# First feed-forward layer by one level of Strassen, second layer in column halves, w_out by token sets

## The chip, the cores and the metric

The kernel runs on one core of one Trainium2 chip. The metric is device time in microseconds (us) of one execution, the median of 3 runs: 1400.36 us for the kernel before (1397.95 to 1401.98). Engines are named as the profile names them: PE (TensorE, matrix products), PEld (its weight loads), DVE (VectorE), ACT (ScalarE), POOL (GpSimd), SP (SyncE, which only issues DMAs here).

## What is computed

One layer of a hybrid decoder on 1024 prompt tokens and 8 sample tokens with the same weights, 1032 tokens together. All data is float32; the model is 1024 wide, the feed-forward layer 2816.

```python
def hybrid_layer(x, h_re, h_im, cbuf, p):
    xn = rmsnorm(x, g_mix)
    z = xn @ w_in
    u, cv, cg = z[..., :512], z[..., 512:1024], z[..., 1024:1536]
    gates = jax.nn.sigmoid(z[..., 1536:])
    y, hr, hi = s5_layer(u, h_re, h_im, ...)
    yg = jax.nn.gelu(y) @ w_glu
    ya = yg[..., :D_MODEL] * jax.nn.sigmoid(yg[..., D_MODEL:])
    c, new_buf = causal_dwconv(cv * jax.nn.sigmoid(cg), cbuf, conv_w, conv_b)
    yb = jax.nn.silu(layernorm(c, ln_g, ln_b)) @ w_pw
    merged = gates[..., :D_MODEL] * ya + gates[..., D_MODEL:] * yb
    x = x + merged @ w_out
    hn = rmsnorm(x, g_ffn) @ w_ff_in
    x = x + (jax.nn.silu(hn[..., :D_FF]) * hn[..., D_FF:]) @ w_ff_out
    return x, hr, hi, new_buf
```

A last rmsnorm with g_final follows. The change touches the last four lines.

## The kernel before

Activations lie transposed, 128 features on the partitions and the 1032 tokens along the free dimension. A factor of a product is scaled by a power of two and split into two float16 numbers, high and low; a product is three passes of matmuls (high by high, weights high by activations low, weights low by activations high), added up in PSUM. `lin` does this for one output tile of 128 features: `wdma` loads the raw weights on SP's queue into one of 3 buffers (`wr`), `wscale` finds the scale (ACT squares and sums, L513; POOL takes the maximum over partitions, L518; DVE makes a power of two, L523, L497, L498, and `invs` its inverse, L508), `wsplit16` splits (ACT makes the high half, L558, DVE the low one, L562), and `mtile` issues the matmuls (L591), three column pieces of 344 for each k and pass, into one of two PSUM buffers of three banks (`mm`).

The stages in order: norm and S5 layer, the input projections, the convolution, the gates with `pw(m)` for m = 0 to 7 (product with w_pw, gating, merged rows `mg`). Then come `wout(m)` and `residual(m)`. `wout` loads and splits one tile of w_out; `residual` loads a tile of x as tokens by features and transposes it on PE (`pxt`, L1084, L1087), and ACT copies it from PSUM (L1085, L1088). The merged rows are split into `mh`. `out(c)` does w_out for one of three column groups of 384, 384 and 264 tokens: `mcol` issues the matmuls (L1120), DVE adds the residual (L1143), squares are summed, and `put` scales by the reciprocal root and by g_ffn (L1156) and splits into `xg` (L1158, L1159).

`ff_in(n)` makes one of 22 tiles of hidden rows: two products of 8 k by 3 passes by 3 pieces, 144 matmuls, with weights of the gate and of the linear half, a sigmoid on ACT (L1206), two multiplications on DVE (L1207, L1210), and a sum of squares. n = 0 is issued by column groups, so that it can begin while `out` ends. The hidden rows of a block are split by `hsplit` when all of them are there, and then used by the second layer: for each m one `lin` over the block's rows, added to `x1` on DVE (L1261). `FBLK` gives the hidden tiles of each of 5 blocks. The first n of the next block is issued between `hsplit` and the second layer of a block. The last block's product (`pfo`, L1278) is done by three column groups with the transposes of the output (`tr`, L1287) and the last norm (L1290 on ACT, L1297 on DVE) behind each.

Each engine works in order. A scheduler sets that order from the program's order; `hp()` and `high_priority` move instructions ahead of others, HPS = 20000 further than HPO = 3000.

Of the kernel before, what the change touches and what calls it, by code (L numbers as in the profile page):

```python
# [437 lines left out]
def hybrid_step(ctx: ExitStack, tc: tile.TileContext, x_prompt, x_sample, state_ssm_re, state_ssm_im,  # L438
# [673 lines left out]
    B3 = (0, 3 * P, 6 * P, TOK)  # L1112
    K3 = ((0, 1, 2), (3, 4, 5), (6, 7, 8))
    G3 = ((0, 1, 2), (3, 4, 5), (6, 7))

    def mcol(w, acts, o):
        n = len(acts)
        for k in range(n):
            for i, (a, b) in enumerate(((0, 0), (0, 1), (1, 0))):
                T.matmul(o, w[a][:, k], acts[k][b], start=(k == 0 and i == 0), stop=(k == n - 1 and i == 2))  # L1120

    wo, so = [], cp.tile([P, 8], F32, name="so")

    def wout(m):
        raw = wdma(w_out, 0, 8, m * P)
        t = pair(sa("wo", (P, 2, 8, P), F16))
        s = wscale([raw], [t[0]], so[:, m:m + 1])
        wo.append(wsplit16(raw, t[0], t[1], s))

    xg = []  # L1130

    def out(c):
        a, b = B3[c], B3[c + 1]
        w = b - a
        inv = io
        sq = sb("sq", (P, 384), tag="t")
        for gr in G3:
            pt = mpsum()
            for i, m in enumerate(gr):
                mcol(wo[m], [(h[:, a:b], l[:, a:b]) for h, l in mh], pt[:, i, :w])  # L1140
                x = x1[m][:, a:b]
                with hp():
                    V.scalar_tensor_tensor(x, pt[:, i, :w], inv[:, m:m + 1], x, MUL, ADD)  # L1143
                    if m == 0:
                        A.activation(sq[:, :w], x, AF.Square)
                    else:
                        t = sb("sqt", (P, 384), tag="t")
                        A.activation(t[:, :w], x, AF.Square)
                        V.tensor_tensor(sq[:, :w], sq[:, :w], t[:, :w], ADD)
        if c == 0:  # L1150
            xg.extend(pair(sb("xgp", (P, 2, TOK), F16, tag="mg")) for _ in range(8))

        def put(o, p):
            for m in range(8):
                t = sb("xgt", (P, 384), tag="t")
                V.scalar_tensor_tensor(t[:, :w], x1[m][:, a:b], gff[:, m:m + 1], p, MUL, MUL)  # L1156
                h, l = xg[m]
                A.copy(h[:, a:b], t[:, :w])  # L1158
                V.tensor_tensor(l[:, a:b], t[:, :w], h[:, a:b], SUB)  # L1159
# [4 lines left out]
    for m in range(3):
        wout(m)
    for m in range(4):
        residual(m)
    mh = [pair(sa("mh", (P, 2, TOK), F16) if m < 5 else sb("mh", (P, 2, TOK), F16, tag="gy")) for m in range(8)]
    with hp():
        msc, mcx = ascale(mss, "msc")  # L1170
        for c in range(3):
            for m in range(8):
# [3 lines left out]
    for m in range(3, 8):  # L1176
        wout(m)
        if m < 7:
            residual(m + 1)
# [156 lines left out]
```

## Time and profile before

| | |
|---|---|
| runs | 1400.36 us median, 1397.95 to 1401.98 |
| profiled execution | 1400.05 us, of it span 1398.3 us |
| mean granted clock of PE | 0.974 |

The span by stages, as the view of windows gives it: the first two columns are the window and its length, then busy us of PE, PEld, DVE, ACT and POOL with the number of instructions, the granted clock of PE as a share of full speed, the DMA engines' busy share, and GB/s.

```profile
85.00:450.00 365.00, 332.92 (x2226) 231.88 (x2226) 310.28 (x595) 145.04 (x265) 38.00 (x64) 0.95 0.39 93
450.00:554.00 104.00, 104.00 (x715) 69.83 (x714) 54.50 (x85) 45.38 (x58) 5.99 (x10) 1.00 0.23 67
704.00:1346.00 642.00, 642.00 (x4389) 430.04 (x4387) 249.32 (x497) 216.38 (x313) 31.33 (x80) 1.00 0.17 50
1346.00:1398.00 52.00, 40.48 (x293) 29.33 (x291) 34.56 (x126) 9.47 (x18) 0.00 (x0) 0.94 0.21 82
```

The windows end where the work changes: the gates and w_pw from 450 to 554 us, w_out with n = 0 of the first layer from there to 704, both feed-forward layers to 1346, the last block's second layer with the output behind it. In a row of the timeline the first number is the start, the second the duration; in a group of instructions the two numbers behind the first bar are busy us in all and the mean ns of one, and behind the second bar stands the idle time ahead of them with what ended it.

### The profile page before, as it was taken

To read this page: it belongs to the slowest core of one execution; us is meant where nothing else is said; L and a number is where in the kernel's file an instruction comes from. 1 tells how busy PE (TensorE), PEld (TensorE's weight loads), DVE (VectorE), ACT (ScalarE), POOL (GpSimd) and SP (SyncE) were. 2 spreads that over 40 slices of the span, in tenths; PEclk is the share of its full clock that TensorE was granted. 3 is DMA by queue.
4 is the path that set the end of the run, shared out by engine and by line. 5 is a ranking of instruction groups with operands and counts; after the bars stand their busy time and mean duration, and the time that the engine had idled before them with its cause. 6 is when DMAs were issued, how large, how long until landed. Compare 5 with 4: busy or idle time off the path is not lost.

```text
span 1398.3 us, 22132 instructions
## 1 busy us (share of the span) xinstructions
PE 1303.8 (93%) x8877; PEld 892.6 (64%) x8877; DVE 800.6 (57%) x1830; ACT 535.3 (38%) x882; POOL 98.9 (7%) x208
## 2 busy tenths in 40 slices
PE   3898798999998999599989999999999999999996
PEld 2776565666665666367656666666666666666665
DVE  5976888989996635646532433335432434342547
ACT  5834333453334434822332422324232422342412
POOL 5000001100010000000000000000000000000100
PEclk9999899999998999799999999999999999999999
DMA  7445754341121115320011112111221112110103
GB/s 191 126 96 119 141 109 107 99 115 37 55 63 45 31 57 145 117 61 1 1 50 51 29 54 76 46 41 32 65 62 54 29 54 76 46 49 27 50 27 122
DMA packets 168976, 96.45 MB, mean 69 GB/s; under 512 B 12799, under 2 KB 165003, under 8 KB 168873
## 3 DMA queue, kind: packets, MB, share of 16 engines
q1 hardware_dynamic: 167469, 92.44, 24.3%
q0 software_dynamic: 896, 1.63, 0.6%
q8 instruction: 69, 1.13, 0.3%
q10 hardware_dynamic: 507, 0.97, 0.3%
q14 instruction: 35, 0.28, 0.1%
HBM read 76.72 MB, written 9.65 MB: 62 GB/s over the span
## 4 chain that ended last, share of the span: by engine, by line
PE 70%; DVE 14%; issue 9%; DMA 3%; ACT 1%; POOL 1%; SPq 1%; DVEq 0%; ACTq 0%; POOLq 0%
PE mm L591 57%; PE mm L1120 7%; DVE acc L895 3%; PE pfo L1278 2%; PE pu L731 2%; DVE wl L562 2%; DMA Y<-X 1%; DVE tb L895 1%; POOL sv L518 1%; DMA U<-ud 1%; DVE mg L968 1%; DMA M<-kvd 1%; DVE mg L965 0%; DVE xgt L1156 0%; PE ptr L721 0%
## 5 line engine op out<-in xcount | busy, mean ns | idle before, releaser
L591 PEld LDWEIGHTS <-wh 128*128 128x128 f16 x4656 | 457.5, 98 | 234.2 <-issue 5.4
L591 PE MATMUL mm<-xgp,wh 128*128 128x344 f16 x2016 | 350.6, 310 | 4.5 <-DVE py L497 4.5
L591 PEld LDWEIGHTS <-wl 128*128 128x128 f16 x2328 | 228.8, 98 | 112.3 <-issue 0.8
L513 ACT ACTIVATE wh<-wr 128x1024 bf16<-128x1024 f32 (+2 forms) x114 | 109.1, 957 | 407.0 <-PE mm L591 264.4
L591 PE MATMUL mm<-xn,wh 128*128 128x344 f16 (+2 forms) x1152 | 205.6, 313 | 1.9 <-ACT ut L743 1.1
L591 PE MATMUL mm<-xgp,wl 128*128 128x344 f16 x1008 | 202.7, 310 | 0.0
L562 DVE SCALAR_TENSOR_TENSOR wl<-wr,wsc,wh 128x1024 f16<-128x1024 f32 (+2 forms) x112 | 129.8, 1160 | 63.7 <-ACT wh L558 61.2
L558 ACT ACTIVATE wh<-wr,wsc 128x1024 f16<-128x1024 f32 (+2 forms) x112 | 117.0, 1045 | 116.5 <-DVE wsc L498 109.4
L591 PE MATMUL mm<-hp,wh 128*128 128x344 f16 x912 | 157.8, 309 | 0.0
L518 POOL PARTITION_ALL_REDUCE sv<-wss x124 | 67.1, 541 | 1088.6 <-ACT wh L513 1038.8
L523 DVE TENSOR_SCALAR sv<-sv 128x1 f32<-128x1 f32 x124 | 18.9, 152 | 180.7 <-POOL sv L518 180.7
L591 PE MATMUL mm<-xn,wl 128*128 128x344 f16 (+2 forms) x576 | 118.7, 313 | 0.0
L1210 DVE SCALAR_TENSOR_TENSOR g<-mm,inv,g 128x1032 f32<-128x1032 f32 x21 | 27.2, 1293 | 127.2 <-PE mm L591 127.2
L1120 PE MATMUL mm<-mh,wo 128*128 128x384 f16 (+1 forms) x576 | 90.3, 319 | 3.9 <-DVE x L1143 2.8
L591 PE MATMUL mm<-hp,wl 128*128 128x344 f16 x456 | 91.3, 309 | 0.0
L1261 DVE SCALAR_TENSOR_TENSOR x<-mm,inv,x 128x1032 f32<-128x1032 f32 x32 | 41.3, 1292 | 72.3 <-PE mm L591 72.3
L1120 PEld LDWEIGHTS <-wo 128*128 128x128 f16 x576 | 57.7, 101 | 35.3 <-issue 8.9
L591 PE MATMUL mm<-gyp,wh 128*128 128x344 f16 x384 | 66.6, 309 | 1.4 <-DVE mg L968 0.8
L895 DVE SCALAR_TENSOR_TENSOR acc<-t,cws,acc 128x511 f32<-128x511 f32 (+14 forms) x60 | 44.9, 749 | 0.0
L895 DVE SCALAR_TENSOR_TENSOR acc<-c,cw,acc 128x511 f32<-128x511 f32 (+14 forms) x60 | 43.6, 746 | 0.0
L591 PE MATMUL mm<-gyp,wl 128*128 128x344 f16 x192 | 38.4, 309 | 0.0
L1278 PE MATMUL pfo<-hp,wlp 128*128 128x392 f16 (+2 forms) x216 | 34.1, 309 | 0.0
(379 smaller groups left out, 1401.5 us busy)
## 6 DMA issues: line engine op xcount, KB each, us to landing
wr<-in_w_ff_in_dram SPq DMA_DIRECT2D x44, 512.0 KB
wr<-in_w_in_dram SPq DMA_DIRECT2D x28, 512.0 KB
wr<-in_w_ff_out_dram SPq DMA_DIRECT2D x24, 320.0 KB
...
```

The lines of the kernel that those rows point to most:

```text
L513: A.activation(junk, src, AF.Square, accum_out=o)
L518: GP.partition_all_reduce(v, ss, P, RMAX)
L523: V.tensor_scalar(v, v, 1e-28, None, MAXI)
L558: A.mul(hi, raw, s)
L562: V.scalar_tensor_tensor(lo[:, sl], raw[:, sl], s, hi[:, sl], MUL, SUB)
L591: T.matmul(pt[:, c, :b - a], ww[:, k], aa[:, a:b], start=(k == 0 and i == 0), stop=(k == n - 1 and i == 2))
L731: T.matmul(o, ww[:, k], aa[:, c0:c0 + w], start=(k == 0 and i == 0), stop=(k == 7 and i == 2))
L895: V.scalar_tensor_tensor(o[:, q:], x[:, 0:HT - q], w[q], o[:, q:], MUL, ADD)
L1120: T.matmul(o, w[a][:, k], acts[k][b], start=(k == 0 and i == 0), stop=(k == n - 1 and i == 2))
L1210: V.scalar_tensor_tensor(c3(g1), z, inv, c3(g1), MUL, MUL)
L1261: V.scalar_tensor_tensor(c3(x1[m]), z, inv, c3(x1[m]), MUL, ADD)
L1278: T.matmul(pt[:, :w], wl[m][a][:, k], hid[k][b][:, c0:c0 + w], start=(k == 0 and i == 0), stop=(k == nb - 1 and i == 2))
```

## The change

**w_out.** `wout(0)` to `wout(3)` and `residual(0)` to `residual(3)` are issued inside the pw loop, and all eight split tiles stay in SBUF. The PSUM pool `mm` ends behind the pw loop; three buffers of two banks (`mq`) take its place. The 1032 tokens are seen as two halves of 516. A token set j is 129 tokens of the first half and the same 129 of the second, 258 columns in a matmul; `msplit(j)`, `out(j)` and `xsplit(j)` split, multiply and rescale one set. `xsplit` also forms the sums of activations that Strassen needs, and splits all into float16 tiles `xs`.

**First layer.** The two output tiles of one n (gate, linear) by the two halves of the tokens, with the 1024 features as two halves of 512, make a 2 by 2 block product. `ff_in` does it by 7 products in place of 8: `ff_prep` forms four sums of weight blocks on DVE and splits seven blocks of 512; `prod` issues 4 k by 3 passes by 2 pieces of 258 columns, 24 matmuls; DVE adds the products into the hidden tiles (L1270), ACT copies the first (L1298). n = 0 does two column pieces, 387 and 129 of each half.

**Second layer.** Two halves of 516 columns in pieces of 258. The blocks change, the first n of the next block comes ahead of `hsplit`, and some tags get other buffers. The factor of a bound (32, now 64) allows for the sums.

```diff
+    def wout(m):
+        raw = wdma(w_out, 0, 8, m * P)
...
     def pw(m):
...
-        with hp():
+        with tc.high_priority(offset=HPS if m == 7 else HPO):
...
         pw(m)
+        if 2 <= m < 6:
+            wout(m - 2)
+        if m >= 4:
+            residual(m - 4)
+    emm.close()
+    emq = ctx.enter_context(ExitStack())
+    mq = emq.enter_context(tc.tile_pool(name="mq", bufs=3, space=bass.MemoryType.PSUM))
...
+    msplit(0)
+    for m in range(4, 8):
+        residual(m)
+    for m in range(4, 8):
+        wout(m)
...
+    def out(j):
+        n = 2 * (SETS[j + 1] - SETS[j])
+        ms_ = (5, 4, 6, 7, 0, 1, 2, 3) if j else range(8)
+        for i in range(4):
+            pt = qpsum()
+            for b in range(2):
+                m = ms_[2 * i + b]
...
+                o = v2(pt[:, b, :n])
+                for k in range(8):
+                    for q, (u, v) in enumerate(((0, 0), (0, 1), (1, 0))):
+                        T.matmul(o, wo[m][u][:, k], cset(mh[k][v], j), start=(k == 0 and q == 0),
+                                 stop=(k == 7 and q == 2))
...
+    def xsplit(j):
...
+            V.scalar_tensor_tensor(k[:, 0:2], cset(x1[m], j), gff[:, m:m + 1], rb, MUL, MUL)
+            V.scalar_tensor_tensor(k[:, 2:4], cset(x1[m + 4], j), gff[:, m + 4:m + 5], rb, MUL, MUL)
+            V.tensor_tensor(t[:, 0], k[:, 1], k[:, 0], SUB)
+            V.tensor_tensor(t[:, 1], k[:, 3], t[:, 0], SUB)
+            V.tensor_tensor(t[:, 2], k[:, 3], k[:, 1], SUB)
+            V.tensor_tensor(t[:, 3], k[:, 2], t[:, 1], SUB)
+            for x, src in ((xs[m][0][:, :, m % 2:m % 2 + 1, cs], k[:, 0:1]), (xs[m][1][:, :, :, cs], k[:, 2:4]),
+                           (xs[m][2][:, :, :, cs], t[:, 0:2]), (xs[m][3][:, :, :, cs], t[:, 2:4])):
+                A.copy(x[:, 0], src)
+                V.tensor_tensor(x[:, 1], src, x[:, 0], SUB)
...
+    def ff_prep(n):
+        r1, r2 = (wdma(w_ff_in, 0, 8, c0 + n * P) for c0 in (0, DFF))
+        s = wscale([r1, r2], [junk.rearrange("p (k m) -> p k m", k=8)] * 2)
...
+            V.tensor_tensor(s1, a21, a22, ADD)
+            V.tensor_tensor(s2, s1, a11, SUB)
+            V.tensor_tensor(s3, a11, a21, SUB)
+            V.tensor_tensor(s4, a12, s2, SUB)
+            ws = []
+            for src in (a11, a12, s2, s3, a22, s1, s4):
...
+                A.mul(w[:, 0], src, s)
+                V.scalar_tensor_tensor(w[:, 1], src, s, w[:, 0], MUL, SUB)
+                ws.append(w)
...
+            def prod(w, x):
+                o = qpsum()
+                for k in range(4):
+                    i, c = x or (0, k % 2)
+                    for q, (u, v) in enumerate(((0, 0), (0, 1), (1, 0))):
+                        for z, (a, b) in enumerate(pcs):
+                            T.matmul(o[:, z, :w_], w[:, u, k * P:(k + 1) * P], xs[k][i][:, v, c, a:b],
+                                     start=(k == 0 and q == 0), stop=(k == 3 and q == 2))
...
+            c11, c12, c21, c22, u = view(g1), view(g1, 1), view(h2), view(h2, 1), view(g1, 1)
+            pt = prod(ws[0], None)
+            with tc.high_priority(offset=HPS):
+                A.copy(c21, pt)
+            add(c11, prod(ws[1], B21), c21)
+            act(c11, view(sg), c11)
+            add(u, prod(ws[2], T2), c21)
+            add(c22, prod(ws[3], T3), u)
+            add(c21, prod(ws[4], T4), c22)
+            pt = prod(ws[5], T1)
+            add(u, pt, u)
+            add(c22, pt, c22)
+            add(c12, prod(ws[6], B22), u)
+            act(c12, view(sg, 1), c12)
...
     for b in range(len(blocks) - 1):
+        nxt = fill(b + 1, block(b + 1), 1)
         hid, cx = hsplit(cur[1], cur[0])
...
-NBT = {"gy": 4, "mg": 8, "b": 5, "t": 6}
+NBT = {"gy": 4, "mg": 8, "b": 5, "t": 7}
...
-FBLK = [5, 5, 5, 4, 3]
+FBLK = [4, 4, 4, 4, 4, 2]
```

Three places show how the engines' order changes. The first is DVE in the middle of a block of the first layer. In the kernel before, this is half a step (L523 to L498: a scale; L1207: the gate; L562: the low half of a weight tile; names are output, arrow, inputs):

```order
L1207 SCALAR_TENSOR_TENSOR g_991_8805<-mm_8732,inv_8730,s_992_8806 128x1032
L508 TENSOR_SCALAR inv_9010<-wsc_9004,gsc 128x1
L562 SCALAR_TENSOR_TENSOR wl_8998<-wr_8995,wsc_9004,wh_8997 128x1024
L1210 SCALAR_TENSOR_TENSOR g_991_8805<-mm_8826,inv_8824,g_991_8805 128x1032
```

In the changed kernel DVE has, within n = 1, the adds of products from PSUM (`q`, L1270), the low halves of the weight blocks of n = 2 (`ws`, L1249) and the weight sums of n = 3 (`sw`, L1237 to L1240):

```order
L1270 TENSOR_TENSOR g_867_7818<-q_7875,h_868_7819 128x516
L1249 SCALAR_TENSOR_TENSOR ws_8039<-wr_8010,wsc_8022,ws_8039 128x512
L1270 TENSOR_TENSOR h_868_7819<-q_7901,g_867_7818 128x516
L1249 SCALAR_TENSOR_TENSOR ws_8042<-sw_8029,wsc_8022,ws_8042 128x512
L1237 TENSOR_TENSOR sw_8267<-wr_8251 128x512
L1238 TENSOR_TENSOR sw_8268<-sw_8267,wr_8249 128x512
L1239 TENSOR_TENSOR sw_8269<-wr_8249,wr_8251 128x512
L1270 TENSOR_TENSOR h_868_7819<-q_7927,h_868_7819 128x516
L1240 TENSOR_TENSOR sw_8270<-wr_8249,sw_8268 128x512
```

Where one instruction emptied a PSUM buffer for 72 matmuls, one now does for 24, and the first weight sum of the raw tile wr_8251 stands between two of them.

The second place is ACT at the change from one n to the next in the first block. Before, the squares of a raw tile (L513) and the sigmoid that reads PSUM (L1206) alternate:

```order
L558 ACTIVATE wh_7621<-wr_7619,wsc_7628 128x1024
L513 ACTIVATE wh_7715,wss_7717<-wr_7713 128x1024
L1206 ACTIVATE s_830_7524<-mm_7450,inv_7448 128x1032
L558 ACTIVATE wh_7715<-wr_7713,wsc_7722 128x1024
L513 ACTIVATE wh_7807,wss_7809<-wr_7805 128x1024
```

After, from the last sigmoid of n = 1 (L1274) to the first high halves of n = 3 (L1248):

```order
L1274 ACTIVATE sg_7820<-g_867_7818,inv_7787 128x516
L516 ACTIVATE junkw,wss_8493<-wr_8489 128x1024
L1298 COPY h_897_8058<-q_8060 128x516
L1248 ACTIVATE ws_8054<-sw_8031,wsc_8022 128x512
L516 ACTIVATE sg_7820,hss_7558<-g_867_7818 128x1032
L1248 ACTIVATE ws_8275<-wr_8249,wsc_8261 128x512
```

The squares of the raw tile of n = 4 (wr_8489) stand ahead of the copy that takes the first product of n = 2 from PSUM.

The third place is DVE at the end of w_out. Before, the last column group is rescaled (L1156, L1159), and then the multiplications of n = 0 (L1200, L1201) follow:

```order
L1156 SCALAR_TENSOR_TENSOR xgt_7052<-x_682_6160,gt,prb_7019 128x264
L1159 TENSOR_TENSOR xgp_6423<-xgt_7048,xgp_6423 128x264
L1159 TENSOR_TENSOR xgp_6424<-xgt_7052,xgp_6424 128x264
L523 TENSOR_SCALAR sv_7347<-sv_7347 128x1
L497 TENSOR_SCALAR py_7351<-sv_7347 128x1
L1200 SCALAR_TENSOR_TENSOR g_798_7238<-mm_7092,inv_7088,s_799_7239 128x768
```

After, the last rows of `xsplit(3)` (L1217 to L1225; `tk`, `tt` are the scaled rows and their sums) stand in one queue with the adds of n = 0's second column piece (L1270, 129 wide) and the weight work of n = 1 (L1237 to L1249):

```order
L1225 TENSOR_TENSOR xs_6563<-tt_7526,xs_6563 128x2x129
L1219 TENSOR_TENSOR tt_7542<-tk_7541,tt_7542 128x129
L1270 TENSOR_TENSOR g_831_7559<-q_7680,h_832_7560 128x129
L1249 SCALAR_TENSOR_TENSOR ws_7797<-wr_7771,wsc_7783,ws_7797 128x512
L1238 TENSOR_TENSOR sw_7790<-sw_7789,wr_7771 128x512
L1239 TENSOR_TENSOR sw_7791<-wr_7771,wr_7773 128x512
L1249 SCALAR_TENSOR_TENSOR ws_7800<-wr_7771,wsc_7783,ws_7800 128x512
L1225 TENSOR_TENSOR xs_6564<-tt_7526,xs_6564 128x2x129
```

Up to the pw loop PE, DVE, ACT and SP have the same rows in the same order in both kernels.

More of the change, by code (lines that the diff above doesn't have):

```diff
@@ L1088, in residual @@
                 A.copy(xT[:, D:], pt[:, :8])
+    wo, so = [], cp.tile([P, 8], F32, name="so")
+    junk = cp.tile([P, D], BF16, name="junkw")
+    def wout(m):
+        raw = wdma(w_out, 0, 8, m * P)
+        if m == 5:
+            t = [wp.tile([P, 8, P], F16, name=nm(q), tag=q) for q in ("wh", "wl")]
+        else:
+            t = pair(sa("wo", (P, 2, 8, P), F16) if m < 5 else sb("wo", (P, 2, 8, P), F16))
+        s = wscale([raw], [junk.rearrange("p (k m) -> p k m", k=8)], so[:, m:m + 1])
+        wo.append(wsplit16(raw, t[0], t[1], s))
     wpw, mss = [], cp.tile([P, 8], F32, name="mss")
@@ L1111, in hybrid_step @@
         pw(m)
[L1112 to L1145, printed above, removed]
-                    else:
[L1147 to L1159, printed above, removed]
-        with hp():
-            stat_rstd(sq, 1.0 / D, K3[c], put)
@@ L1164, in hybrid_step @@
[L1164 to L1172, printed above, removed]
-                sl = slice(B3[c], B3[c + 1])
-                split(mg[m][:, sl], mh[m][0][:, sl], mh[m][1][:, sl], msc)
[L1176 to L1179, printed above, removed]
@@ new lines, in hybrid_step, with msplit, qset @@
+    with tc.high_priority(offset=HPS):
+        msc, mcx = ascale(mss, "msc")
+    def msplit(j):
+        with tc.high_priority(offset=HPS if j == 0 else 0):
+            for m in range(8):
+                split(cset(mg[m], j), cset(mh[m][0], j), cset(mh[m][1], j), msc)
+    msplit(0)
[3 more added lines that the diff above has]
+        wout(m)
+    io = cp.tile([P, 8], F32, name="io")
+    ssq = sb("ssq")
+    xs, b11 = [None] * 4, []
+    def qset(j):
+        return ssq[:, 2 * SETS[j]:2 * SETS[j + 1]]
@@ L1251, in hybrid_step @@
     for b in range(len(blocks) - 1):
+        nxt = fill(b + 1, block(b + 1), 1)
         hid, cx = hsplit(cur[1], cur[0])
-        nxt = fill(b + 1, block(b + 1), 1 if b < len(blocks) - 2 else 9)
+        if b == len(blocks) - 2:
+            fill(b + 1, nxt, 9)
         if b == len(blocks) - 2:
@@ L1258, in hybrid_step @@
                 wlast(m - 4)
-            z, inv = lin(w_ff_out, m * P, hid, cx, r0=starts[b] * P)
-            with hp():
-                V.scalar_tensor_tensor(c3(x1[m]), z, inv, c3(x1[m]), MUL, ADD)
+            w, ws_ = wload(w_ff_out, starts[b] * P, blocks[b], m * P)
+            inv = invs(ws_, cx)
+            for h in range(2):
+                pt = qpsum()
+                for k in range(blocks[b]):
+                    for q, (u, v) in enumerate(((0, 0), (0, 1), (1, 0))):
+                        for z in range(2):
+                            c0 = 516 * h + 258 * z
+                            T.matmul(pt[:, z, :258], w[u][:, k], hid[k][v][:, c0:c0 + 258],
+                                     start=(k == 0 and q == 0), stop=(k == blocks[b] - 1 and q == 2))
+                x = v2(x1[m][:, 516 * h:516 * h + 516])
+                with hp():
+                    V.scalar_tensor_tensor(x, pt[:, :, :258], inv, x, MUL, ADD)
         if b == len(blocks) - 2:
```

128 lines of the change are left out of this document (93 added, 35 removed).

## The prediction

> **What bounds the kernel now.** I read the page first (busy time, chain), then the stages of 100 us, then the waits of the slow stage.
>
> ```profile
> span 1398.3 us, 22132 instructions
> PE 1303.8 (93%) x8877; PEld 892.6 (64%) x8877; DVE 800.6 (57%) x1830; ACT 535.3 (38%) x882; POOL 98.9 (7%) x208
> PE 70%; DVE 14%; issue 9%; DMA 3%; ACT 1%; POOL 1%; SPq 1%; DVEq 0%; ACTq 0%; POOLq 0%
> ```
> ```profile
> 500.00:600.00 100.00, 84.03 (x526) 54.44 (x525) 51.85 (x103) 59.25 (x104) 5.50 (x14) 0.91 0.38 108
> 800.00:900.00 100.00, 100.00 (x687) 67.10 (x686) 40.20 (x80) 30.61 (x47) 5.18 (x13) 1.00 0.19 56
> 1000.00:1100.00 100.00, 100.00 (x688) 67.08 (x687) 34.20 (x66) 31.81 (x43) 3.85 (x11) 1.00 0.19 54
> ```
>
> TensorE is busy 93% of the span and carries 70% of the chain. A window's columns are busy us of PE, PEld, DVE, ACT, POOL, then the granted clock: from 800 to 1300 us PE is at 100.00 of 100 at clock 1.00, with DVE at 34 to 42. That is the feed-forward: a matmul less there is time less, as long as DVE and ACT keep up. Around w_out (550 to 704) PE waits. The kernel of before took 1400.05 us in the profiled execution (1.75 around the span), beside a median of 1400.36; I sum against 1400.05.
>
> **The first layer, n = 1 to 21.** One n now, and the price of a matmul by its columns:
>
> ```profile
> 905.75 1.29 DVE L1210 SCALAR_TENSOR_TENSOR g<-mm,inv,g 128x1032 f32<-128x1032 f32 x1 [6.09 <-PE mm L591]
> 926.75 1.29 DVE L1210 SCALAR_TENSOR_TENSOR g<-mm,inv,g 128x1032 f32<-128x1032 f32 x1 [6.09 <-PE mm L591]
> ```
> ```profile
> 58.24 2.18 PE pu L731 x20
> 1351.52 1.49 PE pfo L1278 x9
> 1375.38 0.98 PE pfo L1278 x9
> ```
>
> The gate's last multiplication comes every 21.00 us: 144 matmuls of 344 columns, 145.8 ns each. Matmuls of 256 columns run at 2.18/20 = 109.0 ns (pu; pfo gives 0.98/9 = 108.9), of 392 at 1.49/9 = 165.6; that is 0.416 ns a column, so 258 columns take 109.8 ns. After: 7 products of 4 k by 3 passes by 2 pieces, 168 matmuls of 258, 18.45 us. Seven products for eight saves only 12.2% of the time, since short matmuls carry more overhead. **2.55 us by 21 n: -53.6.**
>
> The Trainium skill, "TensorE: Matmul & The Clock Gate", section "Back-to-back issue gap", gives a sustained spacing of 81 ns for 128 columns and 131 for 512; on a straight line between them 258 columns would take about 98 ns (an estimate), some 41 us less over these n. The trace doesn't agree: by that line 344 columns would take 109 ns, and the row has 145.8. I keep the rows.
>
> This holds if DVE, ACT and the loads fit into 18.45 us.
>
> ```profile
> 330.26 0.75 DVE L895 SCALAR_TENSOR_TENSOR acc<-t,cws,acc 128x511 f32<-128x511 f32 x1
> 330.93 0.75 DVE L895 SCALAR_TENSOR_TENSOR tb<-c,cw,tb 128x505 f32<-128x505 f32 x1
> 328.67 1.24 DVE L986 TENSOR_TENSOR lns<-acc,acc 128x1032 f32<-128x1032 f32 x1
> 329.81 0.23 DVE L928 SCALAR_TENSOR_TENSOR rd<-tq,cw,rd 128x8 f32<-128x8 f32 x1
> ```
> ```profile
> 906.99 0.15 DVE L523 TENSOR_SCALAR sv<-sv 128x1 f32<-128x1 f32 x1
> 907.18 0.15 DVE L497 TENSOR_SCALAR py<-sv 128x1 int32<-128x1 int32 x1
> ```
> ```profile
> L562 DVE SCALAR_TENSOR_TENSOR wl<-wr,wsc,wh 128x512 f16<-128x512 f32 x8 | 6.0, 749 | 1.9 <-ACT wh L558 1.8
> L558 ACT ACTIVATE wh<-wr,wsc 128x512 f16<-128x512 f32 x8 | 5.7, 711 | 3.1 <-DVE wsc L498 1.8 <-DVE swl L498 1.3
> L513 ACT ACTIVATE wh<-wr 128x1024 bf16<-128x1024 f32 x82 | 86.4, 1054 | 288.9 <-PE mm L591 164.9 <-issue 116.0 <-DMA wr<-in_w_in_dram 2.9
> L513 ACT ACTIVATION_READ_ACCUMULATOR wh<-wr 128x1 f32 x114 | 21.3, 187 | 0.0
> L1206 ACT ACTIVATE s<-mm,inv 128x1032 f32<-128x1032 f32 x21 | 23.1, 1102 | 0.0
> L1085 ACT COPY x<-pxt 128x512 f32<-128x512 f32 x16 | 9.1, 582 | 6.3 <-PE pxt L1084 6.3
> ```
>
> Back to back a 511-wide multiply-add starts 0.67 us before the next, a 1032-wide addition 1.14, so about 0.60 for 512. DVE per n: 7 weight splits of 512 at 0.67 (4.7), 7 adds of product halves of 516 at 0.61 (4.3), 4 weight sums at 0.60 (2.4), two gate products of 516 and one of 1032 (2 x 0.67 + 1.24 = 2.6), 5 small ones (0.19 from start to start, 1.0): 15.0 us, 81% of 18.45; by whole durations (0.75 for a split) about 16.4, 89%. ACT: 7 splits at 0.71, two sums of squares of a raw tile at 1.05 + 0.19, a copy at 0.58, two sigmoids of 516 at about 0.6 and the hidden row's squares at 1.25: 10.5 us. Both fit, but DVE goes from 38% to 81%.
>
> DVE works in order, and two places make it wait. The first weight sum (L1237) stands for the DMA of the second raw tile, which the 3 raw buffers let go only after the second split of the n before; behind it the add of the next product is queued, and PE for that product's PSUM.
>
> ```profile
> 899.69 11.36 SPq L482 DMA_DIRECT2D wr<-in_w_ff_in_dram  x2
> GB/s 0 0 0 0 0 0 0 0 0 5 96 259 341 320 118 0 0 0 0 0 0 0 0 0 0 0 0 0 0 0 0 0 0 98 177 304 346 160 19 0
> ```
>
> SP's queue row covers two loads from 899.69; the second row is 896 to 915 in slices of 0.475 us, so 512 KB issued at 899.69 has landed by 903.1, 3.4 us. Counted from the end of the third product: add and split 1.3, DMA 3.4, against 3.9 at which DVE arrives; three sums later, at 6.5, it takes the fifth product's add, ready at 5.3. 1.2 us late, while three PSUM buffers let PE run two products (5.3 us) ahead. So PE is not stopped. The second place is ACT: at a block's start the sum of squares of a raw tile (L516), itself behind that tile's DMA, stands ahead of the copy of the next n's first product (L1298). From the sixth product's end: two adds 1.2, split 0.7, DMA 3.4, squares 1.25, copy 0.6: 7.2, against 5.3 at which the product is ready and 10.5 at which PE wants its buffer. For such places (6 blocks, twice in the first) the bounds are 0 and a whole round, 3.4 + 1.25 = 4.7 each, 33; I take 1.2 each, **+8**.
>
> **The second layer and the tail.**
>
> ```profile
> L1261 DVE SCALAR_TENSOR_TENSOR x<-mm,inv,x 128x1032 f32<-128x1032 f32 x32 | 41.3, 1292 | 72.3 <-PE mm L591 72.3
> 1360.00:1370.00 10.00, 10.00 (x69) 6.65 (x68) 7.51 (x35) 3.57 (x7) 0.00 (x0) 1.00 0.13 52
> 1370.00:1380.00 10.00, 10.00 (x82) 8.20 (x81) 8.88 (x37) 3.78 (x8) 0.00 (x0) 1.00 0.30 111
> 1380.00:1390.00 10.00, 6.48 (x56) 5.34 (x54) 8.17 (x32) 2.12 (x4) 0.00 (x0) 1.00 0.39 157
> ```
>
> Before, 19 blocks of hidden rows go through L591: 19 x 8 x 9 x 145.8 = 199.5 us. After, 20 in pieces of 258: 20 x 8 x 12 x 109.8 = 210.8. **+11.3**, all on PE. Its 32 additions at L1261 become 80 of half the width; DVE, which waited 72.3 us there, hides that. The last block has 2 rows for 3: PE saves a third of the 216 pfo matmuls, 216 x 146 / 3 = 10.5 us. But from 1360 DVE is at 7.5 to 8.9 of 10: in the later two of three column groups it becomes the bound. The first group's third counts in full (9 x 8 x 165.6 / 3 = 4.0); of the other 6.5 I take 2.5, bounds 0 and 6.5. **-6.5.**
>
> **w_out and n = 0.**
>
> ```profile
> 553.48 0.60 PE L591 MATMUL mm<-chp,wl 128*128 128x344 f16 x3
> 553.92 0.82 PE L1084 MATMUL pxt<-zi,xc 128*128 128x128 f32 x6
> 703.56 11.55 PE mm L591 x61
> ```
> ```profile
> 554.00:704.00 150.00, 126.44 (x821) 83.70 (x820) 85.96 (x217) 65.42 (x129) 4.01 (x12) 0.94 0.17 50
> 560.00:570.00 10.00, 5.82 (x27) 3.23 (x28) 8.47 (x20) 10.00 (x21) 0.36 (x1) 0.83 0.58 176
> 690.00:700.00 10.00, 6.51 (x53) 5.05 (x51) 6.13 (x16) 4.43 (x11) 0.00 (x0) 1.00 0.00 0
> 700.00:710.00 10.00, 6.45 (x28) 3.58 (x29) 6.20 (x14) 5.49 (x8) 0.70 (x2) 0.66 0.19 56
> PE pxt L1087 <- ACT x L1085: 5.8, 6, 3.7
> L591 PEld LDWEIGHTS <-wh 128*128 128x128 f16 x4656 | 457.5, 98 | 234.2 <-issue 5.4
> ```
>
> From the last pw matmul (554) to n = 1 (703.56) are 149.5 us. PE's work at full clock is 192 x (2 x 162.5 + 112.5 ns) = 84.0 for w_out, 10.5 for eight residuals (each 8 transposes, 6 of which take 0.82, and a short one), 21.0 for n = 0: 115.5, so 34 are lost, to ACT's copies, loads, DVE, and clocks of 0.66 to 0.83 behind the waits.
>
> After: 4 of 8 residuals stand in the pw loop (5.2 us of transposes, +5 there; the 4 raw w_out tiles issued there pass SP's queue ahead of the x tiles, with DMA at 0.17 to 0.38 of its share). The split of the last merged tile, its scale and the first token set's halves make a chain of about 7 (multiply-add 1.3, add 1.15, squares 1.25, POOL and five small ones 1.7, split 1.2), in which the other residuals lie. w_out: 8 x 8 x 3 x 4 x 109.8 = 84.5; sums and broadcasts of rows 4; the first 387 columns of n = 0 84 x 163.5 = 13.7, the last 129 between 84 x 56 (columns alone) and 84 x 98 (the weight load's row): 4.7 to 8.2, taken 6.4. Sum 121. Then DVE: the fourth set's rescale is 13 small ones (2.5), 8 multiplications of 258 (0.40 each), 16 subtractions of 129 (0.20) and 16 of 129 or 258 that form low halves (4.9), 15 us with the copies of its sums; 6 more are the adds of n = 0's first piece, against 13.7 of PE under it: PE waits about 8; and the last piece's products, 0.8 us each, come faster than DVE's adds between the splits of n = 1: about 8. 137 in all, **-13**. Bounds: no waits, 121 (-29); as much lost as now, 5 + 5 + 109 + 34 = 153 (+3).
>
> **Sum:** 1400.05 - 53.6 + 8 + 11.3 - 6.5 - 13 = **1346 us.** With the bounds: 1322 without any wait (-8 and -16), 1387 with stalls of 33 and w_out's +3.
>
> **Rivals.**
> *No waits at all*: PE-bound everywhere, 1322. The dense stage of before ran at 100.00 with DVE at 40%; against it, DVE at 81%.
> *Half given back*: DVE by whole durations, 89%, and each late load pushing the next; 1.8 us per n, 1346 + 21 x 1.8 = 1384 less a few already counted: 1380. For it: each n has two queues with 1 to 3 us of slack.
> *Lock step, slower than before*: if DVE falls more than two products (5.3 us) behind, PE waits for each product's add before it gets a buffer: 7 x 0.61 = 4.3 us per n. 1338 (without my +8) + 21 x 4.3 = 1428. It decides where loads land 3 us later than the 3.4 of the row, in nearly every n. Against it: 3 us of slack, DMA at 0.2 of its share.
> *The clock*: after short idles PE is granted less (0.83 and 0.66 above). If the change of PSUM buffer at every product (2.64 us; 72 matmuls and 10.5 us before) left gaps that halve the clock for half of each product, 21 x 18.45 / 2 = 194 more, 1540. The dense windows, which cycle two buffers, show 1.00. The Trainium skill, same page, section "A second HAM failure mode: psum-queue depth-cycling", describes such an oscillation with buffers changed at each group; no run here shows it.
>
> **How the numbers follow.** Forecast (1333 to 1360) 0.52; no waits 0.15; half given back (1360 to 1395) 0.21; within 0.3% of before, about what a measurement can tell from no change, 0.03; lock step 0.07; clock 0.02. Faster 0.88, same 0.03, slower 0.09. Range 1320 to 1385: it leaves out the slower cases, the upper end of "half given back" and a little below.
>
> **What would show it.** The combining adds on DVE every 18.4 to 18.9 us per n at the same place; PE at 100 of 100 with clock 1.00 in the dense windows; DVE at 75 to 85 there; waits of PE on the adds of under 15 us in all; n = 1 starting 131 to 145 us after 554; the second layer's matmuls at 110 ns. Wrong it would be if PE waits for the adds (L1270) in each n, or if matmuls of 258 columns, two runs of 129 in w_out, take more than 110 ns.

## The result, and the profile after

The changed kernel takes 1365.58 us (median of 4 runs, 1363.99 to 1369.8), the kernel before 1401.17 (1397.95 to 1402.61): a ratio of 0.9754, 95% interval 0.9725 to 0.9782, or 35.6 us less. The profiled execution took 1366.18 us, its span 1364.1.

The page of the changed kernel (span, busy us of the engines, chain), then three of its windows of 100 us with the same columns as before:

```profile
span 1364.1 us, 25399 instructions
PE 1263.1 (93%) x10083; PEld 1001.7 (73%) x10083; DVE 1036.5 (76%) x2402; ACT 621.6 (46%) x1118; POOL 102.8 (8%) x198
PE 51%; DVE 26%; issue 9%; DMA 8%; ACT 4%; POOL 1%; SPq 1%; DVEq 0%; ACTq 0%; POOLq 0%
```
```profile
800.00:900.00 100.00, 97.94 (x880) 84.88 (x879) 75.08 (x146) 48.77 (x81) 4.16 (x10) 1.00 0.19 54
1000.00:1100.00 100.00, 98.36 (x884) 85.30 (x882) 70.44 (x142) 46.71 (x81) 5.21 (x13) 1.00 0.20 58
1100.00:1200.00 100.00, 100.00 (x903) 87.19 (x901) 73.23 (x148) 45.19 (x77) 4.83 (x12) 1.00 0.18 54
```

PE's share of the chain fell from 70% to 51%, though it is as busy as before: DVE, which carried 14%, carries 26%, DMA, which carried 3%, carries 8%, and a window that was at 100.00 now often ends at 98. A busy DVE alone does not slow PE (from 1100 to 1200 us DVE is at 73 and PE at 100.00); what the missing 2 us are is seen in the waits of PE from n = 1 to the end of the second layer (who waited, for whom, us in all, times, longest):

```profile
PE q L1291 <- DVE h L1270: 4.5, 7, 1.2
PE q L1291 <- ACT h L1298: 4.5, 5, 1.1
```

Behind all twelve of these waits stands a load. On ACT, the sum of squares of a raw tile (L516) waits for the tile and holds up the copy of a product; on DVE the first weight sum waits, and the next product's add behind it (timelines of ACT and DVE: start, duration, what; in brackets the idle time before it and what ended it):

```profile
847.87 1.06 ACT L516 ACTIVATE junkw<-wr 128x1024 bf16<-128x1024 f32 x1 [2.70 <-DMA wr<-in_w_ff_in_dram]
848.84 0.19 ACT L516 ACTIVATION_READ_ACCUMULATOR junkw<-wr 128x1 f32 x1
848.93 0.57 ACT L1298 COPY h<-q 128x516 f32<-128x516 f32 x1
```
```profile
855.01 0.74 DVE L1249 SCALAR_TENSOR_TENSOR ws<-sw,wsc,ws 128x512 f16<-128x512 f32 x1
858.31 0.69 DVE L1237 TENSOR_TENSOR sw<-wr 128x512 f32<-128x512 f32 x1 [2.55 <-DMA wr<-in_w_ff_in_dram]
859.04 0.69 DVE L1238 TENSOR_TENSOR sw<-sw,wr 128x512 f32<-128x512 f32 x1
859.65 0.69 DVE L1239 TENSOR_TENSOR sw<-wr,wr 128x512 f32<-128x512 f32 x1
860.26 0.68 DVE L1270 TENSOR_TENSOR h<-q,h 128x516 f32<-128x516 f32 x1
```

By stages, from the starts of PE's matmuls in the two traces (the last pw matmul at 553.8 before and 557.0 after; n = 1; the first `pfo`; the end of the span):

| stage | before | after | difference | forecast |
|---|---|---|---|---|
| up to n = 1 | 703.56 | 703.23 | -0.3 | -13 |
| first and second layer | 643.0 | 616.5 | -26.5 | -34.3 |
| last product and output | 51.7 | 44.4 | -7.3 | -6.5 |
| span | 1398.3 | 1364.1 | -34.2 | -53.8 |

So 13 of the 20 us that are missing were lost ahead of n = 1. The windows of the changed kernel there, from the last pw matmul to n = 1:

```profile
557.00:586.00 29.00, 19.44 (x148) 15.04 (x146) 25.25 (x65) 25.73 (x58) 2.74 (x2) 0.94 0.27 76
586.00:661.00 75.00, 75.00 (x670) 64.03 (x669) 54.54 (x190) 26.82 (x69) 0.57 (x3) 1.00 0.08 22
661.00:684.00 23.00, 19.72 (x117) 11.30 (x116) 21.76 (x76) 10.34 (x26) 0.00 (x0) 1.00 0.00 1
684.00:703.00 19.00, 11.36 (x82) 8.61 (x82) 18.90 (x56) 10.35 (x24) 0.00 (x0) 0.59 0.09 27
```

Only the second of them is limited by PE. In the first, half of the first token set is done in 29 us, with ACT and DVE busy 25 of them; in the last two DVE is busy 40.7 of 42 us, and in the last PE is granted 0.59 of its clock.

### The profile page after: what moved, and what is told of

It reads as the page before. It is cut to its first block, busy times and chain, and to the rows that moved or that the text cites. A ratio compares the mean times of both kernels' runs of the same rounds, so it can differ in the third digit from the quotient of the medians.

```text
span 1364.1 us, 25399 instructions
## 1 busy us (share of the span) xinstructions
PE 1263.1 (93%) x10083; PEld 1001.7 (73%) x10083; DVE 1036.5 (76%) x2402; ACT 621.6 (46%) x1118; POOL 102.8 (8%) x198
## 4 chain that ended last, share of the span: by engine, by line
PE 51%; DVE 26%; issue 9%; DMA 8%; ACT 4%; POOL 1%; SPq 1%; DVEq 0%; ACTq 0%; POOLq 0%
PE q L1291 18%; PE q L1370 12%; PE mm L594 10%; PE q L1177 5%; DMA wr<-in_w_ff_in_dram 5%; DVE acc L898 4%; PE pu L734 2%; DVE ws L1249 2%; DVE wl L565 2%; DVE tb L898 1%; DMA Y<-X 1%; POOL sv L521 1%; ACT ws L1248 1%; DVE g L1270 1%; DVE mh L609 1%
## 5 line engine op out<-in xcount | busy, mean ns | idle before, releaser
L1291 PE MATMUL q<-xs,ws 128*128 128x258 f16 (+2 forms) x3696 | 422.6, 275 | 18.7 <-DVE xs L1225 6.7
L1291 PEld LDWEIGHTS <-ws 128*128 128x128 f16 x3696 | 358.4, 98 | 81.7 <-issue 24.6
L594 PEld LDWEIGHTS <-wh 128*128 128x128 f16 x1728 | 169.5, 98 | 86.2 <-issue 5.1
L1370 PE MATMUL q<-hp,wh 128*128 128x258 f16 x1280 | 193.5, 272 | 0.0
L1370 PEld LDWEIGHTS <-wh 128*128 128x128 f16 x1280 | 124.0, 97 | 18.1
L561 ACT ACTIVATE wh<-wr,wsc 128x512 f16<-128x512 f32 (+1 forms) x76 | 70.0, 922 | 126.9 <-DVE wsc L501 122.6
L1370 PE MATMUL q<-hp,wl 128*128 128x258 f16 x640 | 122.5, 273 | 0.0
L594 PEld LDWEIGHTS <-wl 128*128 128x128 f16 x864 | 85.2, 99 | 41.3 <-issue 0.3
L516 ACT ACTIVATE wh<-wr 128x512 bf16<-128x512 f32 (+1 forms) x78 | 65.0, 833 | 107.6 <-PE q L1370 44.6
L516 ACT ACTIVATE junkw<-wr 128x1024 bf16<-128x1024 f32 x52 | 54.8, 1054 | 109.2 <-DMA wr<-in_w_ff_in_dram 101.6
L565 DVE SCALAR_TENSOR_TENSOR wl<-wr,wsc,wh 128x512 f16<-128x512 f32 (+1 forms) x76 | 75.9, 999 | 22.6 <-ACT wh L561 22.4
L1374 DVE SCALAR_TENSOR_TENSOR x<-q,inv,x 128x516 f32<-128x516 f32 x80 | 59.9, 750 | 35.8 <-PE q L1370 35.6
L1177 PE MATMUL q<-mh,wo 128*128 128x258 f16 x672 | 80.0, 275 | 7.5 <-ACT mh L608 4.2
L1249 DVE SCALAR_TENSOR_TENSOR ws<-sw,wsc,ws 128x512 f16<-128x512 f32 x88 | 64.7, 744 | 19.4 <-ACT ws L1248 18.4
L1248 ACT ACTIVATE ws<-sw,wsc 128x512 f16<-128x512 f32 x88 | 62.3, 715 | 28.9 <-PE q L1291 28.8
L1370 PEld LDWEIGHTS <-wl 128*128 128x128 f16 x640 | 61.9, 97 | 9.0
L1249 DVE SCALAR_TENSOR_TENSOR ws<-wr,wsc,ws 128x512 f16<-128x512 f32 x66 | 48.7, 744 | 17.9 <-ACT ws L1248 17.6
```

The costliest lines, as they stand in the source:

```text
L516: A.activation(junk, src, AF.Square, accum_out=o)
L561: A.mul(hi, raw, s)
L565: V.scalar_tensor_tensor(lo[:, sl], raw[:, sl], s, hi[:, sl], MUL, SUB)
L594: T.matmul(pt[:, c, :b - a], ww[:, k], aa[:, a:b], start=(k == 0 and i == 0), stop=(k == n - 1 and i == 2))
L1177: T.matmul(o, wo[m][u][:, k], cset(mh[k][v], j), start=(k == 0 and q == 0), stop=(k == 7 and q == 2))
L1248: A.mul(w[:, 0], src, s)
```

## Experiments

Each is the changed kernel with one edit, unless said otherwise. Stage times are taken from the trace as in the table above: "first layer" is the time in which PE goes from n = 1 to the last block without the second layer (403.4 us in the changed kernel, 3528 matmuls, 114.4 ns each; the second layer 213.1, 1920 matmuls, 111.0 ns each), "w_out stretch" the time from the start of the last pw matmul to that of n = 1's first (146.2 us). Apart from the kernels of three and four changes, each ran once. In the seven kernels whose edit leaves the first layer alone it took 400.2 to 402.5 us, so the 403.4 is the longest of eight, and about 3 us of any difference from it is scatter. The w_out stretch took 145.8 and 146.3 us in the two kernels that leave it alone.

### One scale for all n

```diff
-        s = wscale([r1, r2], [junk.rearrange("p (k m) -> p k m", k=8)] * 2)
-        inv = invs(s, gsc[:, 2:3])
+        if not once:
+            so1 = cp.tile([P, 1], F32, name="so1")
+            once.append(wscale([r1, r2], [junk.rearrange("p (k m) -> p k m", k=8)] * 2, so1))
+            once.append(invs(once[0], gsc[:, 2:3], "inv1", 1))
+        s, inv = once
```

> All n of the first layer use the scale of n = 0; the sums of squares of their raw tiles and the maxima on POOL are left out (the scale is a power of two, so only the precision changes). Theory: of the 9 us that PE waits in the first layer behind n = 1, about half stand behind such squares on ACT, which wait for their tile's load; 4 to 5 us less, with no wait of PE on the copy L1298. The other half, DVE's first weight sum waiting for its load, stays. Rival: the waits only move to the next thing that the load holds up (the splits); then less than 1.5 us.

1351.96 us. The first layer falls from 403.4 to 392.4 us, 111.2 ns a matmul, and no wait of PE is left from n = 1 on. Not half but all of the loss, 11 us against the changed kernel's trace and 8 to 10 against the seven others, hung on the squares. DVE still waits for loads; only PE no longer does. DVE's waits for loads from 704 to 1300 us, in the changed kernel and in this one:

```profile
DVE sw L1237 <- DMA wr<-in_w_ff_in_dram: 46.6, 20, 3.9
```
```profile
DVE sw L1240 <- DMA wr<-in_w_ff_in_dram: 33.5, 19, 4.3
```

33.5 us of waits on DVE that cost PE nothing: the room in DVE's queue and in three PSUM buffers covers them, as forecast, as long as ACT isn't held up too. The changed kernel's trace fits this: five of PE's seven waits for DVE's add come 11 to 12 us behind a wait for ACT's copy, and the other two are 0.3 and 0.2 us long. The same windows as above, at 100.00:

```profile
800.00:900.00 100.00, 100.00 (x903) 87.27 (x902) 76.77 (x124) 42.65 (x67) 1.90 (x6) 1.00 0.18 54
1000.00:1100.00 100.00, 100.00 (x904) 87.23 (x902) 74.39 (x129) 39.59 (x64) 2.45 (x7) 1.00 0.20 59
```

This run takes away two things, the squares' own time on ACT and their wait for the load. The next one takes away the waits alone.

### The second raw tile in another buffer

```diff
-        r1, r2 = (wdma(w_ff_in, 0, 8, c0 + n * P) for c0 in (0, DFF))
+        r1 = wdma(w_ff_in, 0, 8, n * P)
+        if n < 2:
+            r2 = wdma(w_ff_in, 0, 8, DFF + n * P)
+        else:
+            with hp():
+                r2 = sa("wr", (P, 8, P))
+                SY.dma_start(r2, w_ff_in[0:D, DFF + n * P:DFF + n * P + P].rearrange("(t p) m -> p t m", p=P))
```

> From n = 2 on the second raw tile of the first layer is loaded into one of the large activation buffers that are free there, so that the ring of 3 raw buffers holds the first tiles alone; the squares are computed as in the changed kernel. Theory (the waits in the first layer come from loads that are issued late, because a raw buffer is let go late): PE's 11 us lost from n = 1 to the last second layer fall under 3, as in the run with one scale, first layer 392 to 395 us for 403, time 1356 or less. Rival (what the run with one scale saved was the squares' own 2.5 us per n on ACT): 8 us or more stay lost.

1359.01 us. The first layer takes 395.9 us: 7.5 of the 11 us are back with all squares still computed (4 to 7 against the seven others), and 3.5 stay lost, a little more than the theory's 3. ACT's waits for the tiles it squares, from 704 to 1300 us, were 97 us in the changed kernel (the first row) and are 4.7 here (the second). DVE's waits for loads, 46.6 us in the changed kernel, fell as well (the third), so this run does not tell the two engines apart. One wait of PE is left, 2.2 us for a weight split (the last row):

```profile
ACT junkw L516 <- DMA wr<-in_w_ff_in_dram: 97.0, 32, 5.3
```
```profile
ACT junkw L516 <- DMA wr<-in_w_ff_in_dram: 4.7, 4, 1.5
DVE sw L1244 <- DMA wr<-in_w_ff_in_dram: 3.5, 4, 1.0
PE q L1297 <- ACT ws L1254: 2.2, 1, 2.2
```

Late loads behind a ring of 3 raw buffers are the cause of more than half of the loss; the squares' own time can account for 3.5 us at most.

### Weight sums twice, with one scale

```diff
+            for _ in range(1 + (n > 0)):
-            V.tensor_tensor(s1, a21, a22, ADD)
+             V.tensor_tensor(s1, a21, a22, ADD)
...
```

> The kernel with one scale for all n (1352, first layer 111.2 ns a matmul), in which DVE forms the four weight sums twice from n = 1 on: 2.4 us more on DVE per n of 18.7. Theory (DVE is not the bound of the first layer, only loads made it wait): PE loses under 3 us in the first layer. Rival (little room is left on DVE, so that the changed kernel stands near the edge): over 10 us lost, 0.5 us or more per n.

1357.66 us. The first layer takes 394.6 us, 2.2 more than without the second sums, although DVE's busy time from 703 to 1304 us grew from 443.0 to 483.5:

```profile
800.00:900.00 100.00, 100.00 (x902) 87.12 (x901) 83.59 (x144) 41.05 (x65) 2.13 (x6) 1.00 0.20 57
1000.00:1100.00 100.00, 99.95 (x901) 86.98 (x900) 79.45 (x146) 37.80 (x64) 3.19 (x9) 1.00 0.19 57
```

DVE at 79 to 84 of 100 still does not hold PE. The rival "half given back", so far as it had DVE's load as its reason, is out.

### Widths of a matmul

```diff
+        wd = (256, 257, 260, 264, 258)[b]
...
-                            c0 = 516 * h + 258 * z
-                            T.matmul(pt[:, z, :258], w[u][:, k], hid[k][v][:, c0:c0 + 258],
+                            c0 = min(516 * h + 258 * z, TOK - wd)
+                            T.matmul(pt[:, z, :wd], w[u][:, k], hid[k][v][:, c0:c0 + wd],
```

> Second layer with pieces of 256, 257, 260, 264 and 258 columns in blocks 0 to 4 (2 or 1 columns of each piece left out in the first two blocks; in blocks 2 and 3 the last piece is displaced and some columns are multiplied twice), everything else as in the changed kernel. If the spacing is 0.416 ns a column through 109.0 at 256: 109.0, 109.4, 110.6, 112.3 and 109.8. Rival: a piece is rounded up to a multiple of 4 columns: 109.0, 110.6, 110.6, 112.3, 110.6; to a multiple of 8: 109.0, 112.3 for all others. Rival: the changed kernel's 111.0 has nothing to do with the width (PSUM banks, weight loads); then 256 also stands at about 110.2.

1362.72 us. Windows of 40 us inside the second layer's five blocks; PE is never idle, and the count behind its busy time is that of the matmuls:

```profile
780.00:820.00 40.00, 40.00 (x367) 35.47 (x366) 24.15 (x55) 15.43 (x29) 2.68 (x6) 1.00 0.27 80
899.00:939.00 40.00, 40.00 (x363) 34.91 (x361) 24.71 (x56) 15.37 (x30) 2.20 (x7) 1.00 0.27 80
1018.00:1058.00 40.00, 40.00 (x361) 34.55 (x359) 24.83 (x56) 15.46 (x30) 2.70 (x7) 1.00 0.27 79
1137.00:1177.00 40.00, 40.00 (x355) 34.10 (x354) 24.55 (x55) 15.29 (x30) 3.00 (x7) 1.00 0.26 77
1275.00:1315.00 40.00, 40.00 (x363) 34.91 (x361) 26.49 (x72) 17.44 (x35) 5.25 (x11) 1.00 0.16 48
```

A window also counts the matmuls that run across its edges, so the spacing is better taken from start to start. The means of 383 pairs are 109.6 ns at 256 columns, 111.0 at 257 and at 258, 111.7 at 260, 113.4 at 264. None of the rules fits: there is a step of 1.4 ns from 256 to 257, none to 258, and then about 0.4 ns a column. Most of the step is in every second spacing, the one from a weight tile's second piece to the next weight tile's first (110.5 to 112.8 ns; between two pieces on the same weights 108.9 to 109.1). Half of what my price missed (109.8 for 111.0) is that step; the rest is that 256 columns themselves take 109.6 in a long run and 109.0 in the short runs that I had read.

### The w_out tiles and residuals behind the pw loop

```diff
-        if 2 <= m < 6:
-            wout(m - 2)
-        if m >= 4:
-            residual(m - 4)
...
     msplit(0)
+    for m in range(4):
+        wout(m)
+        residual(m)
```

> The four w_out tiles and four residuals that the change put into the pw loop are issued behind it again, in between the first token set's halves and the other four. Theory (moving them is worth what it takes from PE, 5 us of transposes, and the wait for four loads): the last pw matmul ends 3 to 4 us earlier than 557.3, but n = 1 starts 8 to 15 us later than 703.2, time 1375 to 1380. Rival (the end of w_out is set by DVE's work in xsplit, so what stands before it is worth little): n = 1 starts within 3 us of 703.

1375.54 us, n = 1 at 716.0. The last pw matmul starts at 551.4 instead of 557.0, but the w_out stretch takes 164.6 us instead of 146.2. Moving this work into the pw loop is worth 12.8 us, as the first theory had it.

### The rest of the residuals in the pw loop, too

```diff
-            residual(m - 4)
+            residual(2 * m - 8)
+            residual(2 * m - 7)
...
-    for m in range(4, 8):
-        residual(m)
```

> All eight residuals are issued in the pw loop (two behind each of the last four pw) and none behind it. Theory (the first token set takes 21 us because transposes, their copies on ACT and the w_out tiles stand between its halves): the last pw matmul ends 5 us later, the first set takes 5 to 10 us less, and n = 1 starts 0 to 5 us earlier than 703.2; time 1361 to 1366. Rival (loads: 2 MB more ahead of the last w_out tiles): the w_out tiles come later and n = 1 starts later.

1361.12 us, n = 1 at 700.8. The w_out stretch takes 143.9 us, 2.3 less. The last pw matmul is not later: 41 of the 72 transposes still stand behind it on PE, ahead of the first set. So the first set starts at 570.8 for 564.2, and then runs densely; w_out ends at 662.5 for 663.9.

### Weight work of n = 0 later

```diff
-    ready = [ff_prep(0)]
     out(0)
...
         if j:
             out(j)
+        if j == 1:
+            ready = [ff_prep(0)]
```

> The weight work of n = 0 is issued behind the second token set of w_out instead of ahead of the first; nothing else changes. Theory: in the changed kernel the first weight sum on DVE (at 569.45) and the squares of a raw tile on ACT (at 570.22) stand in the queues ahead of the halves of the first token set and of the last w_out tiles, so the first set takes 21 us for 10.7 us of matmuls; without them the dense part of w_out starts 3 to 5 us earlier than 585.6 and the run takes about 1362 us. Rival: the late w_out tiles and the copies of x hold it up anyway; then the start stays within 1 us of 585.6 and the time at 1366.

1367.58 us. The theory fell: w_out runs on without gaps from 584.5 us, 1 us earlier than before, but at half clock until 589, and n = 1 starts at 708.3, 5.1 us later (the w_out stretch, with the last pw matmul 2.2 us earlier, takes 153.5 us). One transpose waits 2.8 us for ACT's copy, and then PE runs 10 us at half clock:

```profile
580.00:590.00 10.00, 8.93 (x44) 6.46 (x43) 3.19 (x5) 4.66 (x11) 0.00 (x0) 0.53 0.18 52
```

That is the smaller part of the 5.1 us: w_out ends at 665.3 for 663.9, and from there to n = 1 it takes 43.0 us for 39.4. Why the end got longer was not tested; the weight work that was moved now stands nearer to it.

### Halves of sets 1 to 3 later

```diff
-                split(cset(mg[m], j), cset(mh[m][0], j), cset(mh[m][1], j), msc)
+                split(cset(mg[m], j), cset(mh[m][0], j), cset(mh[m][1], j), msc if j == 0 else late[0])
...
     out(0)
+    late.append(cp.tile([P, 1], F32, name="late"))
+    with hp():
+        V.tensor_scalar(late[0], x1[3][:, 0:1], 0.0, msc, MUL, ADD)
```

> The halves of token sets 1 to 3 (24 splits on ACT and on DVE, some 10 us of either) are made to wait for the fourth output tile of set 0, through a scale that is computed again from a value of that tile; nothing is left out. Theory (the first token set takes 29 us from the last pw matmul because ACT and DVE are full there, 25.7 and 25.3 of 29): the dense part of w_out starts 3 to 6 us earlier than 29 us behind the last pw matmul, and n = 1 comes 3 to 5 us earlier, about 142 behind it. Rival (the order of what is left, residual copies and late w_out tiles, holds it up as much): within 1.5 us of 146.

1365.99 us, and this theory fell as well: the last pw matmul starts at 553.1 for 557.0, but n = 1 at 705.9, 2.7 us later, so the w_out stretch takes 152.9 us. Again transposes wait for copies (6.7 us in six waits, for 2.2 in six), and the clock halves:

```profile
580.00:590.00 10.00, 5.98 (x27) 4.10 (x28) 8.98 (x21) 10.00 (x25) 0.00 (x0) 0.50 0.18 53
```

That ACT and DVE are full in these 29 us is thus not shown to be why the first set is late. What is left in their way is put in another order, and the waits of PE that come of it, with the half clock behind them, cost more than the work moved gained.

### POOL for the sums of activations

```diff
-            V.tensor_tensor(t[:, 0], k[:, 1], k[:, 0], SUB)
+            GP.tensor_tensor(t[:, 0], k[:, 1], k[:, 0], SUB)
...
```

> The 16 subtractions of 129 columns per token set that form the sums of activations are done by POOL instead of DVE. Theory (from the end of w_out to n = 1, 663.9 to 703.2, DVE's work sets the pace): DVE has 3.2 us less per set, and the stretch gets 2 to 3 us shorter, if POOL does one in under 0.5 us. Rival (the order and the waits among PE, ACT and DVE set it, or POOL's steps lie in the chain): the stretch is no shorter, or longer by up to 5 us.

1365.14 us, the w_out stretch 146.6 for 146.2: nothing gained. PE's order changed, too: the last 24 matmuls of w_out start at 670.9, behind the first of n = 0. DVE was rid of the subtractions (283 ns each), POOL takes about 550 for one, and DVE's own subtractions became slower while POOL ran. From 640 to 703 us, first the changed kernel, then this one (busy us, mean ns):

```profile
L1225 DVE TENSOR_TENSOR xs<-tt,xs 128x258 f16<-128x258 f32 x24 | 10.0, 419 | 0.8 <-ACT xs L1224 0.8
L1225 DVE TENSOR_TENSOR xs<-tk,xs 128x129 f16<-128x129 f32 x11 | 3.1, 284 | 0.0
```
```profile
L1225 DVE TENSOR_TENSOR xs<-tt,xs 128x258 f16<-128x258 f32 x24 | 11.3, 490 | 0.0
L1220 POOL TENSOR_TENSOR tt<-tk 128x129 f32<-128x129 f32 x10 | 5.5, 550 | 0.0
L1225 DVE TENSOR_TENSOR xs<-tk,xs 128x129 f16<-128x129 f32 x11 | 4.5, 413 | 0.0
```

### Low halves of the fourth set by ACT

```diff
-                V.tensor_tensor(x[:, 1], src, x[:, 0], SUB)
+                if j == 3:
+                    A.copy(x[:, 1], src)
+                else:
+                    V.tensor_tensor(x[:, 1], src, x[:, 0], SUB)
```

> In the fourth token set's rescale the low halves are copies of the scaled rows made by ACT, in place of DVE's subtractions (so these columns' low halves are other numbers); DVE has 16 instructions, 4.9 us, less between 661 and 703, and POOL nothing to do. Theory (DVE's work sets the pace there): from the last pw matmul to n = 1 146.2 us become 141 to 142. Rival (PE, at half clock in the second column piece, sets it): within 1 us of 146.

1356.52 us, the w_out stretch 140.3: 5.9 less for the 16 instructions taken from DVE, 4.9 us by their spacing and 6.2 by whole durations. DVE's work sets the pace from 661 to 703. The rival, PE at half clock, did not hold these 6 us: the last window is 14 us and still at 0.63.

```profile
684.00:698.00 14.00, 11.20 (x89) 8.24 (x89) 13.30 (x39) 13.09 (x40) 0.00 (x0) 0.63 0.08 23
```

### Three changes together

The second raw tile in an activation buffer, all residuals in the pw loop, and the second layer in pieces of 344 again:

```diff
-            for h in range(2):
+            for e, nz in ((0, 2), (2 * CH, 1)):
...
-                        for z in range(2):
-                            c0 = 516 * h + 258 * z
-                            T.matmul(pt[:, z, :258], w[u][:, k], hid[k][v][:, c0:c0 + 258],
+                        for z in range(nz):
+                            c0 = e + CH * z
+                            T.matmul(pt[:, z, :CH], w[u][:, k], hid[k][v][:, c0:c0 + CH],
```

> Three things together: the second raw tile in an activation buffer (alone 1359.0), all residuals in the pw loop (alone 1361.1), and the second layer in three pieces of 344 columns again (two in one PSUM buffer, one in the next). Theory: the gains lie in different stages and add up: 7.5 us in the first layer, 2 to 4 at w_out, and in the second layer 20 x 8 x (12 x 111.0 - 9 x 145.8 ns) = 3.2 us; about 1351 to 1354. Rival: the second layer's unequal PSUM buffers (6 matmuls for 3 per k) make PE wait for DVE, or the first layer's loads collide with it; then 1356 or more.

1351.19 us (median of 4, 1348.53 to 1352.96), 0.9668 of the kernel before (0.9644 to 0.9691). The changed kernel's own ratio, on another chip, is 0.9754 (0.9725 to 0.9782); the intervals don't meet. The first layer takes 394.2 us (-9.2), the second 210.0 (-3.1: 1440 matmuls at 145.8 ns), and n = 1 starts at 700.5 (-2.8). They add up, as forecast (1351 to 1354), since they lie in different stages.

With the late halves of sets 1 to 3 as a fourth change:

> The same late splits in the kernel of three changes (1351.2, n = 1 at 144.3 us behind the last pw matmul, where the residuals are already out of the first set's way). Theory: ACT's first 30 us get shorter here too, n = 1 at 140 to 142, time 1347 to 1349. Rival (with the residuals gone only the chain and half clock behind the wait are left): 1350 to 1352.

1354.23 us (1353.3 to 1355.13), 0.9685 (0.9668 to 0.9701); the w_out stretch is 144.8 us where three changes gave 144.3. No gain, as alone; the two intervals of the ratio overlap.

## Why the prediction was right, and where its terms were off

**The direction, the mechanism and the range were right**: the first layer is bound by PE, its 7 products at 258 columns are cheaper than 8 at 344, and the time lies between 1320 and 1385. The forecast of 1346 was 20 us too low: 1365.58 lies outside the band that I thought likeliest (1333 to 1360, 0.52), in the one that I had given to "half given back" (0.21), though not by that rival's cause, DVE's load. Of my own signs two came out against me: matmuls of 258 columns take 111.0 to 111.2 ns, and 112.0 in the dense part of w_out, where more than 110 was to mean that I was wrong, and n = 1 starts 149 us behind 554 and not 131 to 145.

**First layer.** Forecast 21 x 18.45 + 8 = 395.5 us, measured 403.4. 3528 matmuls at 111.2 ns make 392.4 (for 387.5 at my 109.8: +5); the stalls were 11 us for 8 in this trace, and 8 to 10 in the seven other kernels, at the two places named (ACT's copy L1298 behind the squares, DVE's adds behind the first weight sum), 4.5 us of recorded waits each. I had judged that DVE's place would cost PE nothing; it does cost, but, as far as the run with one scale shows, only together with ACT's.

**Second layer.** Forecast +11.3, measured 213.1 - 199.5 = +13.6, by the matmul's price alone. Together that is 10 us more than forecast; the stage table has 8, because the kernel before took 443.5 us for n = 1 to 21 and not the 441 of 21 x 21.00. **Last product and output:** -6.5 forecast, -7.3 measured.

**w_out and n = 0** is the term that failed: -13 forecast, -0.3 measured. In my sum of 137 us from 554:
- pw loop: 5 us later forecast, 3.2 measured.
- "A chain of about 7, in which the other residuals lie", then 84.5 us of w_out at full pace. The chain was 7.2 (557.0 to 564.2), but of the five residuals behind the last pw matmul only two lay in it, and the first set lost time to transposes, w_out tiles and halves: w_out ran from 564.2 to 663.9, 99.7 us, against 88.5 with its row sums. That is +11, the largest single miss. About 1.7 of it is the matmul's price (112.0 ns in the dense part for 109.8). Moving all residuals brought the end of w_out 1.3 us nearer to the last pw matmul (and n = 1 2.3); two attempts to clear ACT and DVE put it further away. What the other 8 hang on is still open.
- The end: 36 us forecast for the fourth set's rescale and n = 0, 39.4 measured (663.9 to 703.2). That DVE sets the pace there is shown by the run with ACT's low halves. The stretch got shorter in that run with PE's clock still at 0.63, so the half clock, which my sum had left out, was not what held these 6 us; what a full clock would bring there was not tested.

**The rivals.** "No waits" is what the run with one scale does in the first layer. "Half given back" (1380 against 1366) was a little nearer than my forecast, by luck: it put 1.8 us per n into the first layer for DVE's load and late loads; late loads cost 0.5 there, doubled sums on DVE added 2.2 us in all, and most of the miss lies in w_out. "Lock step" did not come: the waits for loads from n = 1 to the end of the second layer end 3.7 to 4.6 us behind the load's issue, not 3 us later than the row's 3.4. For "the clock", the changed kernel's window from 1100 to 1200 has 100.00 at clock 1.00 with a PSUM buffer changed at every 24 matmuls; the oscillation that the Trainium skill describes ("TensorE: Matmul & The Clock Gate", section "A second HAM failure mode: psum-queue depth-cycling") does not appear in this trace's dense stage.
